# Order of work at the norms of a two-layer decoder trunk: hi products first, second transposes later, attention's delays 2.6/2.3 to 2.2/2.7

## The chip, the cores and the metric

The kernel runs on one core of one Trainium2 chip. The metric is the time of one execution on the device, in microseconds (us). TensorE (PE) does the products, VectorE (DVE) and ScalarE (ACT) the elementwise work, GpSimd (POOL) some small vector work, and SyncE (SP) issues most DMA transfers. "PEld" is TensorE's weight load, which runs beside its products.

## The reference, cut to what matters

The trunk has two layers over 256 tokens of width 1024. Each layer is an FFN, a mixer and a second FFN, each followed by a residual and a layer norm:

```
for l in range(DEPTH):                       # DEPTH = 2, x: (256, 1024) float32
    h = swiglu(x, w1[l,0], w3[l,0], w2[l,0]);  x = layernorm(ALPHA*x + 0.5*h)
    h = mixer(x, l, ...);                      x = layernorm(ALPHA*x + h)
    h = swiglu(x, w1[l,1], w3[l,1], w2[l,1]);  x = layernorm(ALPHA*x + 0.5*h)
```

`swiglu` is `(silu(x @ w1) * (x @ w3)) @ w2` with a hidden width of 2816. The mixer projects x to seven parts of width 1024 (u, v, q, k, val and two gates), runs a chunked spatial gate on u and v and a differential attention (8 heads, two score maps of head dimension 64 each, their difference applied to values of width 128) on q, k and val, and merges both through gates and two more weight matrices.

## The kernel before, in words

**Arithmetic.** Every float32 operand of a large product is split into a hi part, a reduced-precision copy that ScalarE writes, and a lo part, the rest, that VectorE writes. A product is then three: w_hi by x_hi, w_lo by x_hi, w_hi by x_lo. `three` (L271) issues them in that order. There x is the stationary operand (a 128x128 weight load for each product) and 512 columns of a weight matrix stream past it. `rows_b` does this for two slices of 128 along the contraction: six products, in the order hi-hi, lo-hi, hi-lo for the first slice, then the same for the second.

**A norm.** The tokens lie in two blocks of 128 (t = 0, 1), each with two halves of 512 columns (h = 0, 1). `finish_s` ends the statistics of a block and normalises it on VectorE (L556, second half first). The half h = 1 goes through ScalarE's `planes` (L184) and a DMA transpose on SP's queue (L189) to the tile `sent`; the half h = 0 goes through four transposes on TensorE (L633). `turn` then scales on ScalarE (L638, after a copy at L628 for h = 1), writes the hi part of x (ScalarE, L233) and the lo part (VectorE, L234), each for four slices of 128 in one instruction. The products of the next stage use x as soon as both are there: `gemm_b2` runs t = 0 with h = 0, then t = 0 with h = 1, then t = 1 in the same way, 24 products for each of these four. Five norms are followed by another stage: three that end an FFN and two that end a mixer. The sixth ends the kernel.

**What sets the order.** TensorE's order is that of the program text (`manual_schedule`). Side work is placed in it by a count of beats: each group of products adds to a clock (`beat`: 0.5 for six products of `rows_b`, and in `gemm_a2` 0.65 for eight of 512 columns and 0.35 for eight of 256), and a task, a generator, runs on when the clock has reached the time that its last `yield` asked for. `turned` is such a task: `waits[0]` beats after the norm of its block it does h = 0 (the four transposes), and `waits[1]` beats after that h = 1. On the other engines a planner orders the instructions: it simulates the engines and gives a free engine the most urgent of its instructions that is ready, where urgency follows the program text (`soon` raises it) and `behind` pins an instruction after another one on its engine.

**Attention.** The mixer computes q and k for two heads at a time (`rope`, four pairs `hp`, each q or k a `gemm_a2` of 2 beats), and after them the gates (eight more `gemm_a2`). Beside them runs, for each pair, the task `attend`, 3.9 beats after its k: scores of the second token block (L838), 0.6 beats later the scores of the first, their softmax (L846, L848) and the difference of the two maps (L857), then a delay, the transposes of the weights on TensorE (L872, L877) and their copies (L874, L879), a second delay, the products with the values (L885, L887), a copy (L890) and four squares (L895) on ScalarE that read and write the PSUM bank, then on GpSimd the norm's inverse root and later a packing and a DMA transpose. These small products share four PSUM banks (`side`).

Of the kernel before, what the change touches and what calls it, by code (L numbers as in the profile page):

```python
# [20 lines left out]
P = 128  # L21
# [3 lines left out]
KT = D // P  # L25
# [33 lines left out]
def trunk(ctx, tc, x, xT, w13a, w13b, w2s, w2p, wb, wqk, wa, wbr, wo, gateb, sgug, sgub, sguwT, sgubias, lam, diffg,  # L59
          lng, lnb, lngT, lnbT, cosT, sinT, out):  # L60
    nc = tc.nc
    V, A, G, PE = nc.vector, nc.scalar, nc.gpsimd, nc.tensor
# [19 lines left out]
    def bank():  # L82
        return psum.tile([P, 512], F32, tag="main", name=name("bank"))

    def side_bank():
        return psum.tile([P, 512], F32, tag="side", name=name("sbank"))
# [12 lines left out]
    def parts(f):  # L99
        return (lambda k: f(k)[:, :T]), (lambda k: f(k)[:, T:])  # L100
# [27 lines left out]
    def beat(w):  # L128

        clock[0] += w  # L130
        for task in list(tasks):
            if task[0] <= clock[0]:
                turn(task)

    def turn(task):
        try:
            task[0] = clock[0] + next(task[1])
        except StopIteration:
            tasks.remove(task)
# [11 lines left out]
    def behind(ins):  # L151

        return tc.issue_after(ins) if ins is not None else nullcontext()

    def stream(src, width=CH, sub=HC, lent=(), after=(None, None)):

        step()
        raw = raw_pool.tile([P, CH], F32, tag="raw", name=name("raw"))  # L160
        nc.sync.dma_start(raw[:, :width], src)
        out = []
        for o in range(0, width, HC):
            if o // HC in lent:
                hi, lo = ([act.tile([P, 512], F32R, tag="slot", name=name(n)) for _ in range(2)] for n in ("lhi", "llo"))
                at = [(hi[j], lo[j]) for j in range(2)]
            else:
                hi = hi_pool.tile([P, HC], F32R, tag="hi", name=name("whi"))
                lo = lo_pool.tile([P, HC], F32R, tag="lo", name=name("wlo"))
                at = [(hi[:, p : p + sub], lo[:, p : p + sub]) for p in range(0, HC, sub)]  # L170
            for p, (h, w) in zip(range(0, HC, sub), at):
                r = raw[:, o + p : o + p + sub]
                with behind(latest[0] if o // HC in lent else early[0] or latest[0]):
                    copied = A.activation(h, r, AF.Copy)  # L174
                if o // HC in lent:
                    early[0] = copied.ins
                with behind(after[o // HC] or latest[1]):
                    V.tensor_tensor(out=w, in0=r, in1=h.bitcast(F32), op=ALU.subtract)  # L178
            out.append((hi, lo))
        return out  # L180
# [37 lines left out]
    def rest_of(pre, after):  # L218

        (_, hi0, lo0), (raw, hi1, lo1) = pre  # L220
        lows(pre[1], after)
        hi = hi_pool.tile([P, HC], F32R, tag="hi", name=name("whi"))
        lo = lo_pool.tile([P, HC], F32R, tag="lo", name=name("wlo"))
        for p in range(0, HC, 512):
            r, h, w = (v[:, o + p : o + p + 512] for v, o in ((raw, HC), (hi, 0), (lo, 0)))
            with behind(early[0]):
                A.activation(h, r, AF.Copy)
            with behind(after):
                V.tensor_tensor(out=w, in0=r, in1=h.bitcast(F32), op=ALU.subtract)
        return [(hi0[:2], lo0[:2]), (hi0[2:], lo0[2:])], [(hi1, lo1), (hi, lo)]  # L230
# [37 lines left out]
    def three(ps, xh, xl, w_hi, w_lo, start, stop):  # L268

        for n, (w, xx) in enumerate([(w_hi, xh), (w_lo, xh), (w_hi, xl)]):  # L270
            PE.matmul(ps, xx, w, start=start and n == 0, stop=stop and n == 2)  # L271
# [30 lines left out]
    def rows_b(ps, t, k0, piece, xh, xl, kts, c0=0, n=512):  # L302

        hi, lo = piece
        for j in range(2):
            k, o = k0 + j, j * 512 + c0
            wh, wl = (w[j][:, c0 : c0 + n] if isinstance(w, list) else w[:, o : o + n] for w in (hi, lo))
            three(ps[:, :n], xh(k)[:, t * P : (t + 1) * P], xl(k)[:, t * P : (t + 1) * P], wh, wl,
                  k == 0, k == kts - 1)
        beat(n / 1024)  # L310

    def rows_p(ps, t, q, piece, xh, xl, c0=0, n=512, stop=False, start=False):

        for j, k in enumerate(q):
            wh, wl = (v[:, j * 512 + c0 : j * 512 + c0 + n] for v in piece)
            three(ps[:, :n], xh(k)[:, t * P : (t + 1) * P], xl(k)[:, t * P : (t + 1) * P], wh, wl,
                  start and j == 0, stop and j == 1)
        beat(n / 1024)
# [58 lines left out]
    def gemm_b2(srcs, xh, xl, done, norm=None):  # L377

        lent, after = [()] * 4, [(None, None)] * 4
        if norm:
            lent = [(0, 1), (0,), (), ()]
            after[1:3] = [(norm.ends[0], norm.ends[0])] * 2
        ps = [[bank() for _ in range(2)] for _ in range(NT)]
        got = [[None] * 4 for _ in range(2)]
        for t in range(NT):
            for c in range(2):
                if norm:
                    norm.ready(t, c)  # L390
                    after[3] = [norm.ends[1]] * 2
                for m in range(2):
                    n = 2 * c + m
                    if t == 0 and n < 2 and norm and norm.pre:
                        if n == 0:
                            got[0][:2], got[1][:2] = rest_of(norm.pre, norm.ends[0])
                    elif t == 0:
                        got[m][2 * c : 2 * c + 2] = stream(srcs[m][:, c * CH : (c + 1) * CH], sub=512, lent=lent[n],
                                                           after=after[n])
                    for i in range(2 * c, 2 * c + 2):  # L400
                        rows_b(ps[t][m], t, 2 * i, got[m][i], xh, xl, KT)
            early[0] = None
            with behind(latest[0] if t == 0 else None):
                done(t, ps[t])
# [246 lines left out]
    def ffn(l, f, i, norm, following=None):  # L651
# [59 lines left out]
        if norm is None:  # L711
            gemm_first([w13b[l, f, 0, 0], w13b[l, f, 1, 0]], front(0))
        else:
            gemm_b2([w13b[l, f, 0, 0], w13b[l, f, 1, 0]], xh, xl, front(0), norm=norm)
# [17 lines left out]
        def plain_pair(n):  # L732
            q = PQ[n]
            w = stream(w2p[l, f, n])
            for c in range(2):
                for t in range(NT):
                    for ps, o, m in ends[t, c]:
                        rows_p(ps, t, q, w[c], hh, hl, o, m, start=q == PQ[0] and t + c == 2)
# [50 lines left out]
    def mixer(l, i, norm):  # L789
        xh, xl = parts(both)  # L790
# [5 lines left out]
        def got_val(t, ps):  # L796
            for h in range(2):
                A.activation(val[t][:, h], ps[h], AF.Copy)

        gemm_b2([wb[l, VAL_, 0], wb[l, VAL_, 1]], xh, xl, got_val, norm=norm)  # L800

        hb = slots("hb", 2 * KT, F32R)
# [21 lines left out]
        def attend(hp, qT, kT):  # L824
# [27 lines left out]
            def less(t, pp):  # L852

                nk = (t + 1) * P
                for j in range(2):
                    s = slice(j * nk, (j + 1) * nk)
                    V.scalar_tensor_tensor(out=pp[0][:, s], in0=pp[1][:, s], scalar=c4[:, t * 2 + j : t * 2 + j + 1],  # L857
                                            in1=pp[0][:, s], op0=ALU.mult, op1=ALU.add)
                return pp[0]
# [4 lines left out]
            V.reciprocal(out=rc, in_=sums[:, 4:])  # L864
            V.scalar_tensor_tensor(out=c4, in0=rc, scalar=neg_lam[l], in1=sums[:, :4], op0=ALU.mult, op1=ALU.mult)
            second, first = less(1, second), less(0, first)
            yield 2.6
            b = side_bank()
            for j in range(2):
                for c in range(2):  # L870
# [6 lines left out]
                PE.transpose(b[:, j * P : (j + 1) * P], first[:, j * P : (j + 1) * P], ident)  # L877
            aT0 = slots("aT", 2)[0][:, :T]
            A.activation(aT0, b[:, :T], AF.Copy)  # L879
            yield 2.3  # L880
            b = side_bank()
            for j in range(2):
                h = hp * 2 + j
# [9 lines left out]
            for q in range(4):  # L893
                s = slice(q * P, (q + 1) * P)
# [8 lines left out]
            for q in range(4):  # L903
                t, j = q // 2, q % 2
# [9 lines left out]
            for j in range(2):  # L914
                h, s = hb[hp * 2 + j], slice(j * T, (j + 1) * T)
# [10 lines left out]
        for br, sec in ((0, GA_), (1, GB_)):  # L926
            gt = slots("gate", KT)
            gates.append(gt)
            for c in range(KT // 2):
                (_, b), = gemm_a2([wa[l, sec, c]], both, lambda m: t512("gz"), lambda: t512("r"))  # L930
                for n in range(2):
                    s = slice(n * T, (n + 1) * T)
# [11 lines left out]
        for t in range(NT):  # L944
# [3 lines left out]
            for h in range(2):  # L948
                s = slice(h * 512, h * 512 + 512)
# [5 lines left out]
        for h in range(2):  # L955
            s = slice(h * 512, h * 512 + 512)
# [46 lines left out]
        ln = Norm(l, i, 2.0 * ALPHA, 4.0 * EPS, m[:, :1])  # L1003

        def done(t, ps):
            for h in range(2):
                ln.part_s(t, h, ps[h], ln.scale)
            ln.finish_s(t, ((2, 1.5), (2, 1))[t])

        gemm_b2([wo[l, 0], wo[l, 1]], view(m_hi), view(m_lo), done)  # L1010
        return ln.close()

    norm = None
    for l in range(DEPTH):
        norm = ffn(l, 0, 0, norm, [wb[l, 1, m] for m in range(2)])
        norm = mixer(l, 1, norm)
        norm = ffn(l, 1, 2, norm, [w13b[l + 1, 0, m, 0] for m in range(2)] if l < DEPTH - 1 else None)
# [92 lines left out]
```

## Time and profile before

| | |
|---|---|
| median of 3 runs | 1212.65 us (1212.43 to 1213.14) |
| the profiled execution: its own time, its span | 1212.84 us, 1211.1 us |
| TensorE busy, products | 1204.1 us, 99% of the span, 5985 products |
| weight loads busy | 1013.1 us, 84% |
| VectorE busy | 944.3 us, 78% |
| ScalarE busy | 857.3 us, 71% |
| GpSimd busy | 91.7 us, 8% |
| moved by DMA | 257.01 MB, 212 GB/s on average |
| granted TensorE clock | full |

How to read it: times in the trace count from the start of the span. Busy shares are over the whole span. Products overlap in the pipeline, so a row of one product of 512 columns shows 0.39 us while such products follow one another more closely. In a row of the timeline stand start, length, engine, line, operation, output and inputs, shapes, the number of merged instructions, and in brackets the idle time ahead of it with what ended it. Engine names that end in q are a sequencer's.

### The profile page before, as it was taken

How to read it: one execution, taken by the hardware profiler on the slowest of the kernel's cores; microseconds unless marked ns; L12 is line 12 of the kernel's file. 1: busy time of each engine (PE TensorE's matmuls, PEld its weight loads, DVE VectorE, ACT ScalarE, POOL GpSimd, SP SyncE). 2: the span in 40 equal slices, each digit the busy share in tenths (PEclk: the TensorE clock that was granted, in tenths of full speed). 3: DMA queues.
4: the chain of work that ended last, by engine and by line, in shares of the span. 5: the costliest groups of instructions: out<-in, count | busy, mean ns of one | idle time of the engine just before them, and what ended most of it. 6: DMA issues, size and time to landing. Idle time of an engine off the chain costs nothing.

```text
span 1211.1 us, 16587 instructions
## 1 busy us (share of the span) xinstructions
PE 1204.1 (99%) x5985; PEld 1013.1 (84%) x5985; DVE 944.3 (78%) x1541; ACT 857.3 (71%) x1384; POOL 91.7 (8%) x184
## 2 busy tenths in 40 slices
PE   9999999999999999999999999999999999999998
PEld 8888888888888878888888888888888888888886
DVE  6658998885796876579985679989756877757798
ACT  6677677679865596776776776776897555767761
POOL 0100000233300000000000000003432000000000
PEclk9999999999999999999999999999999999999999
DMA  8985665655764658566667565765648546687551
GB/s 321 319 265 174 210 251 203 232 176 162 237 223 168 217 165 295 191 187 218 232 215 270 194 180 209 252 226 194 213 141 274 180 174 217 186 275 209 179 203 52
DMA packets 101347, 257.01 MB, mean 212 GB/s; under 512 B 66528, under 2 KB 67600, under 8 KB 74640
## 3 DMA queue, kind: packets, MB, share of 16 engines
q1 hardware_dynamic: 97296, 243.03, 59.9%
q0 software_dynamic: 3536, 12.13, 3.1%
q8 instruction: 47, 0.77, 0.2%
q10 hardware_dynamic: 432, 0.79, 0.2%
q14 instruction: 36, 0.29, 0.1%
HBM read 235.47 MB, written 1.05 MB: 195 GB/s over the span
## 4 chain that ended last, share of the span: by engine, by line
PE 93%; DVE 4%; ACT 2%; issue 1%; DMA 0%; DVEq 0%; ACTq 0%
PE bank L271 35%; PE sbank L271 23%; PE bank L283 17%; PE bank L290 9%; PE sbank L283 2%; PE bank L446 2%; PE sbank L290 1%; PE sbank L838 1%; PE sbank L970 1%; PE sbank L887 1%; DVE nwa L248 0%; ACT xf L638 0%; DVE xtok L556 0%; ACT sq L553 0%; DVE nwy L249 0%
## 5 line engine op out<-in xcount | busy, mean ns | idle before, releaser
L178 DVE TENSOR_TENSOR wlo<-raw,whi 128x1024 fp32r<-128x1024 f32 (+1 forms) x396 | 436.7, 1124 | 144.2 <-ACT whi L174 113.5
L174 ACT ACTIVATE whi<-raw 128x1024 fp32r<-128x1024 f32 (+1 forms) x396 | 372.9, 971 | 125.9 <-PE bank L283 43.3
L271 PE MATMUL bank<-whi,x 128*128 128x512 f32 x840 | 263.4, 390 | 0.0
L271 PEld LDWEIGHTS bank<-whi,x 128*128 128x128 f32 x840 | 157.7, 188 | 32.7
L271 PE MATMUL bank<-wlo,x 128*128 128x512 f32 x420 | 163.6, 390 | 0.0
L271 PE MATMUL sbank<-whi,x 128*128 128x512 f32 x512 | 159.0, 389 | 0.0
L283 PE MATMUL bank<-x,whi 128*128 128x512 f32 x640 | 156.0, 394 | 0.0
L283 PEld LDWEIGHTS bank<-x,whi 128*128 128x128 f32 x640 | 117.2, 188 | 26.3 <-issue 2.3
L271 PEld LDWEIGHTS sbank<-whi,x 128*128 128x128 f32 x512 | 96.1, 188 | 19.9
L353 ACT ACTIVATE shi<-raw 128x1024 fp32r<-128x1024 f32 (+1 forms) x80 | 73.4, 947 | 51.7 <-DVE raw L368 26.4
L271 PE MATMUL sbank<-wlo,x 128*128 128x512 f32 x256 | 99.7, 389 | 0.0
L355 DVE TENSOR_TENSOR slo<-raw,shi 128x1024 fp32r<-128x1024 f32 (+1 forms) x80 | 85.3, 1088 | 14.1 <-ACT shi L353 13.1
L271 PEld LDWEIGHTS bank<-wlo,x 128*128 128x128 f32 x420 | 78.9, 188 | 16.1
L290 PE MATMUL bank<-x,wlo 128*128 128x256 f32 x640 | 85.9, 285 | 0.0
L290 PEld LDWEIGHTS bank<-x,wlo 128*128 128x128 f32 x640 | 81.6, 191 | 2.2
L291 ACT ACTIVATE r<-bank 128x256 f32<-128x256 f32 x112 | 41.5, 376 | 24.7 <-PE bank L290 24.7
L271 PEld LDWEIGHTS sbank<-wlo,x 128*128 128x128 f32 x256 | 48.1, 188 | 9.9
L506 POOL DMA_DIRECT2D bc<-in_lng x6 | 3.2, 529 | 697.0 <-DVE bc L505 697.0
L271 PE MATMUL sbank<-whi,hhi 128*128 128x512 f32 (+1 forms) x144 | 55.5, 386 | 0.0
L271 PE MATMUL sbank<-whi,hlo 128*128 128x512 f32 (+1 forms) x144 | 55.3, 384 | 0.0
L271 PE MATMUL sbank<-wlo,hhi 128*128 128x512 f32 (+1 forms) x144 | 55.2, 384 | 0.0
L702 ACT ACTIVATE planes<-silu 128x1024 uint16<-128x1024 uint16 x40 | 42.0, 1054 | 7.3 <-DVE silu L701 6.2
(248 smaller groups left out, 2012.2 us busy)
## 6 DMA issues: line engine op xcount, KB each, us to landing
raw<-in_w13b SPq DMA_DIRECT2D x76, 1024.0 KB, 5.6
raw<-in_w2p SPq DMA_DIRECT2D x24, 1024.0 KB, 4.8
raw<-in_wa SPq DMA_DIRECT2D x24, 1024.0 KB, 5.3
raw<-in_w2s SPq DMA_DIRECT2D x20, 1024.0 KB, 4.8
raw<-in_wb SPq DMA_DIRECT2D x16, 1024.0 KB, 5.1
raw<-in_wqk SPq DMA_DIRECT2D x16, 1024.0 KB, 4.8
raw<-in_wbr SPq DMA_DIRECT2D x16, 1024.0 KB, 4.9
raw<-in_w13a SPq DMA_DIRECT2D x8, 1024.0 KB, 4.8
```

What stands on the lines that cost most here:

```text
L174: copied = A.activation(h, r, AF.Copy)
L178: V.tensor_tensor(out=w, in0=r, in1=h.bitcast(F32), op=ALU.subtract)
L271: PE.matmul(ps, xx, w, start=start and n == 0, stop=stop and n == 2)
L283: PE.matmul(b[-1], hi[:, k * P : (k + 1) * P], xc(k), start=k == 0, stop=False)
L290: PE.matmul(b[n][:, :T], lo[:, k * P : (k + 1) * P], xc(k)[:, :T], start=False, stop=k == KT - 1)
L291: emptied[0] = A.activation(r[:, s], b[n][:, T:], AF.Copy, scale=scale).ins
L353: A.activation(h, r, AF.Copy)
L355: V.tensor_tensor(out=w, in0=r, in1=h.bitcast(F32), op=ALU.subtract)
L446: PE.matmul(ps[t][m], x[:, j, o + t * P : o + (t + 1) * P], y, start=k0 + j == 0 and o == 0 and y is hi, stop=k0 + j == KT - 1 and y is lo)
L702: A.activation(pk.rearrange("p (w k) -> p w k", w=2), s.bitcast(U16).rearrange("p (k w) -> p w k", w=2), AF.Copy)
L838: PE.matmul(banks[m][:, j * nk : (j + 1) * nk], rows(qT, m, j, t * P, P), rows(kT, m, j, 0, nk), start=True, stop=True)
L887: PE.matmul(b[:, T + j * P : T + (j + 1) * P], aT1[:, (j * 2 + c) * P : (j * 2 + c + 1) * P], v[c], start=c == 0, stop=c == 1)
```

## The change

Three edits. First, at the five norms with a following stage, the first two groups of products (t = 0, the first matrix, slices 0 and 1, then 2 and 3) are issued by a new function: four products with x's hi part (hi and lo weights of both slices), then two with x's lo part. The products are the same twelve. Second, the mixers' norm gives its second block the delays 2.5 and 0.5 beats instead of 2 and 1; the FFNs' norms keep 2 and 1. Third, in `attend` the delay ahead of the transposes is 2.2 beats instead of 2.6, and the one between transposes and values 2.7 instead of 2.3.

```
+    def rows_hl(ps, t, k0, piece, xh, xl, kts):
+        for low in range(2):
+            for j in range(2):
+                k, s = k0 + j, slice(j * 512, (j + 1) * 512)
+                wh, wl = (w[j] if isinstance(w, list) else w[:, s] for w in piece)
+                for w in (wh,) if low else (wh, wl):
+                    PE.matmul(ps, (xh, xl)[low](k)[:, t * P : (t + 1) * P], w, start=not low and k == 0 and w is wh,
+                              stop=False)
+        beat(0.5)
...
     gemm_b2:
-                        rows_b(ps[t][m], t, 2 * i, got[m][i], xh, xl, KT)
+                        (rows_hl if norm and t + n == 0 else rows_b)(ps[t][m], t, 2 * i, got[m][i], xh, xl, KT)
...
     attend:
             second, first = less(1, second), less(0, first)
-            yield 2.6
+            yield 2.2
             b = side_bank()
...
             A.activation(aT0, b[:, :T], AF.Copy)
-            yield 2.3
+            yield 2.7
             b = side_bank()
...
     mixer, done:
-            ln.finish_s(t, ((2, 1.5), (2, 1))[t])
+            ln.finish_s(t, ((2, 1.5), (2.5, 0.5))[t])
```

## The prediction

> **What bounds the kernel now.** I read the page first, then the chain of waits, then the waits that end on TensorE, then the five places where one stage hands its normalised tokens to the next.
>
> ```profile
> span 1211.1 us, 16587 instructions
> ...
> PE 1204.1 (99%) x5985; PEld 1013.1 (84%) x5985; DVE 944.3 (78%) x1541; ACT 857.3 (71%) x1384; POOL 91.7 (8%) x184
> ...
> PE 93%; DVE 4%; ACT 2%; issue 1%; DMA 0%; DVEq 0%; ACTq 0%
> ```
> ```profile
> 28.06 21.76 PE sbank L271 x96
> ```
> ```profile
> PEld bank L271 <- DVE x L234: 2.7, 5, 0.6
> ```
> ```profile
>   DVE xtok L556: 2.1, 4
> ```
>
> The first fence is the page: TensorE is busy for 99% of the span and carries 93% of the chain. The second is a row of the chain: 96 products of 512 columns in 21.76 us, so 0.227 us for one. The third comes from the list of waits: five times TensorE's weight load waits for x's lo part, once at each norm. The fourth is what L633's transposes waited for: the normalised tokens, at two norms (twice each, as weight load and as product). So the end is set by TensorE's own work plus small stalls, and a change of order can earn only stalls.
>
> **The change, part by part.**
>
> *Hi products first.* At the first norm that a mixer follows:
>
> ```profile
> 182.95 0.42 PE L271 MATMUL bank<-lhi,x 128*128 128x512 f32 x1
> 183.06 0.68 DVE L234 TENSOR_TENSOR x<-xf,x 128x512 fp32r<-128x512 f32 x1
> 183.21 0.40 PE L271 MATMUL bank<-llo,x 128*128 128x512 f32 x1
> ...
> 183.79 0.30 PEld L271 LDWEIGHTS bank<-lhi,x 128*128 128x128 f32 x2 [0.62 <-DVE x L234]
> ...
> 187.56 0.39 PE L271 MATMUL bank<-whi,x 128*128 128x512 f32 x1
> ```
>
> Two products with x's hi part run; the third has x's lo part as its weights, and that is not written before 183.06 + 0.68 = 183.74. From 182.95 to 187.56 lie 18 products: 4.61 us where 18 x 0.227 = 4.08 would do, 0.53 lost. Counted back from 187.56 by 16 products, the third really began at 183.93. In the new order lo stands fifth and is due at 182.98 + 4 x 0.227 = 183.89, 0.04 before it can start. Of the 0.53 some 0.08 stays: 0.45 gained. The fourth product now needs the second weight's lo part, which was written before the norm. The list of waits has five such waits, three at norms that an FFN ends.
>
> At a norm that a mixer ends:
>
> ```profile
> 426.38 0.69 DVE L234 TENSOR_TENSOR x<-xf,x 128x512 fp32r<-128x512 f32 x1 [1.43 <-ACT x L233]
> 426.40 0.50 PE L271 MATMUL bank<-lhi,x 128*128 128x512 f32 x1
> ...
> 427.13 0.72 PE L271 MATMUL bank<-lhi,x 128*128 128x512 f32 x2
> ...
> 430.90 0.39 PE L271 MATMUL bank<-whi,x 128*128 128x512 f32 x1
> ```
>
> 18 products take 4.50, 0.42 too long. The first of them is 0.50 long instead of 0.39: 0.11 is a wait for hi, which stays. The other 0.30 is the wait for lo, shorter than the 0.45 by which lo is put off: gained whole.
>
> *The second transposes.* An FFN's norm, then a mixer's:
>
> ```profile
> 188.85 1.00 DVE L556 TENSOR_SCALAR xtok<-xtok,mv,nwy 128x512 f32<-128x512 f32 x2
> ...
> 190.06 0.58 PEld L633 LDWEIGHTS sbank<-ident,xtok 128*128 128x128 f32 x4
> ...
> 190.64 0.49 PE L271 MATMUL bank<-whi,x 128*128 128x512 f32 x1
> ```
> ```profile
> 433.05 1.00 DVE L556 TENSOR_SCALAR xtok<-xtok,mv,nwy 128x512 f32<-128x512 f32 x2
> 433.40 0.39 PE L271 MATMUL bank<-whi,x 128*128 128x512 f32 x1
> ...
> 434.11 0.42 PEld L633 LDWEIGHTS sbank<-ident,xtok 128*128 128x128 f32 x4 [0.74 <-DVE xtok L556]
> ...
> 434.52 0.48 PE L271 MATMUL bank<-whi,x 128*128 128x512 f32 x1
> ```
>
> Undisturbed, the next product follows 0.58 after the transposes' weight load (190.06 to 190.64). In the mixer the load could have begun with the product at 433.40 and the next product came at 434.52, 1.12 later: 0.54 is stall; I take 0.53. The load was 0.71 late, so 0.17 of lateness is absorbed. Half a beat is one group of six products, 1.36 us: the load comes to 433.40 - 0.30 + 1.36 = 434.46, after the 434.11 at which it could start. The stall goes. The total delay of the turn's other half is the same (2.5 + 0.5 = 2 + 1), and that half has no transposes on TensorE.
>
> The FFNs' delays are not changed, and there the first edit makes a new wait: the load comes at 190.06 - 0.45 = 189.61, the tokens are ready at 189.85 + 0.05 = 189.90. Of 0.29 lateness 0.17 is absorbed: 0.12 lost. Behind it on TensorE are only the products of the same norm.
>
> *What is late next in the mixers.* The moved transposes feed the second token block:
>
> ```profile
> 434.80 1.50 ACT L638 ACTIVATE xf<-sbank,ln_b,ln_g 128x128 f32<-128x128 f32 x4
> 436.34 0.63 ACT L233 ACTIVATE x<-xf 128x512 fp32r<-128x512 f32 x1
> 438.28 1.19 ACT L628 ACTIVATE xf<-sent 128x1024 uint16<-128x1024 uint16 x1 [1.31 <-DMA sent<-planes]
> ```
> ```profile
> 438.72 0.39 PE L271 MATMUL bank<-lhi,x 128*128 128x512 f32 x1
> ```
> ```profile
> 1038.73 1.19 ACT L628 ACTIVATE xf<-sent 128x1024 uint16<-128x1024 uint16 x1 [2.82 <-DMA sent<-planes]
> ```
> ```profile
> 1042.30 0.69 DVE L234 TENSOR_TENSOR x<-xf,x 128x512 fp32r<-128x512 f32 x1 [5.67 <-ACT x L233]
> ```
> ```profile
> 1042.87 0.62 PE L271 MATMUL bank<-whi,x 128*128 128x512 f32 x2
> ```
>
> Hi was ready at 436.97, 2.86 after the load at 434.11; after a load at 434.46 it is ready at 437.3, or 437.5 if the longer lag of the FFN holds. TensorE gets to 438.72 - 0.83 = 437.89: 0.4 to 0.6 to spare, and lo, 0.7 later, is just in time. The other half of the block comes through a DMA transpose. In the second layer its lo part ends at 1042.99; its first user is the second product of the last row, at 1043.10, and the first that needs lo stands at 1043.55. With TensorE 0.83 earlier that is 1042.72, but by the lag of the first fence (183.74 to 183.93) lo serves from 1043.18: 0.45 given back. In the first layer the copy comes 1.5 earlier against the same work, and nothing is lost.
>
> *Attention.* TensorE's order is a list of beats: 0.65 for eight products of 512 columns, 0.35 for eight of 256, and a due task runs at the first beat that reaches its time. I added the beats in code order. The first part's end stands at 8.65 beats; +2.6 makes 11.25 and +2.2 makes 10.85, and both are first reached at 11.30. So the transposes do not move at all. The values move instead: from 13.65 (11.30 + 2.3 = 13.60) to 14.00 in the second layer, and in the first, where the floating-point sum falls a hair short of the due time, to 14.65. They hold a PSUM bank until ScalarE has squared it, and two pairs of heads later the scores want it:
>
> ```profile
> 257.31 1.14 PE L838 MATMUL sbank<-qk,qk 64*128 64x256 f32 x8
> ```
> ```profile
> 263.98 0.39 PE L885 MATMUL sbank<-val,aT 128*128 128x128 f32 x2
> ```
> ```profile
> 269.44 0.59 ACT L890 ACTIVATE on<-sbank 128x512 f32<-128x512 f32 x1
> ...
> 272.82 0.26 ACT L895 ACTIVATE sbank<-sbank 128x128 f32<-128x128 f32 x1
> ```
> ```profile
> 272.59 1.80 PE L838 MATMUL sbank<-qk,qk 64*128 64x256 f32 x8
> ```
>
> The scores at 272.59 took 1.80 instead of 1.14: 0.66 lost to the last square. The values before them were done about 265.2, yet their copy went at 269.44 behind another pair's work. Values one beat later (2.77 us, about 268.0) with a copy at once, or one 1.05 us copy later, end their squares between 271.8 and 273.2, as copy to last square takes 3.8: the stall falls to something between 0 and 0.66. By the same lag the pair before it, whose scores at 257.31 wait for nothing, could lose up to 0.7. Bounds of the part: 0.66 gained to 0.7 lost. I take 0.2 gained, as the only wait that the trace shows is one that can shrink.
>
> *The sum.* Three FFN norms: 3 x (0.45 - 0.12) = 1.0. Two mixer norms: 2 x (0.30 + 0.53) - 0.45 = 1.2. Attention 0.2. Together 2.4. The profiled execution took 1212.84 (span 1211.1, 1.7 around it), so 1210.4; it stands 0.2 above the median of the runs, 1212.65, so I forecast **1210.25**.
>
> A page speaks against part of it. The Trainium skill, "DMA: Bandwidth & Descriptors", section "Issuing engines are not separate DMA queues", says that transfers from all engines run on the same 16 DMA engines and interleave. The rows behind it:
>
> ```profile
> 434.70:438.30 3.60, 3.60 (x18) 2.94 (x17) 2.45 (x4) 2.15 (x6) 0.00 (x0) 1.00 1.20 323
> ```
> ```profile
> DMA to landing us min/median/max: 2.7/2.7/5.0
> ```
>
> While the mixer's transpose is in flight the DMA engines carry 323 GB/s (last column of the stretch), and the ten transposes land after 2.7 to 5.0 us. The trace agrees with the page: the 0.45 is a matter of what the transpose meets. With the median landing it is nothing and the sum 2.85; with 5.0 in both layers it is paid twice and the sum is 1.95.
>
> **The rivals.**
>
> *Slower: ScalarE's order at the mixers flips.* ScalarE's instructions are put in order by a planner that fills a gap with whatever it holds ready. For the first block it put the copy of the DMA transpose (L628) right behind the four scalings (L638), ahead of hi:
>
> ```profile
> 420.23 1.06 ACT L184 ACTIVATE planes<-xtok 128x1024 uint16<-128x1024 uint16 x1 [2.73 <-DVE xtok L556]
> ...
> 424.65 1.18 ACT L628 ACTIVATE xf<-sent 128x1024 uint16<-128x1024 uint16 x1
> ```
> ```profile
> 433.63 1.06 ACT L184 ACTIVATE planes<-xtok 128x1024 uint16<-128x1024 uint16 x1 [0.44 <-DVE xtok L556]
> ```
>
> That was 4.4 us after the packing (L184) began; for the second block hi went first, 2.7 after it (433.63 to 436.34). With later transposes that moment comes at about 3.2. If the planner believes the transpose landed by then, L628 goes ahead of hi, and it really waits until 438.28 and 1038.73. Hi then starts at 439.5 and 1039.9 and serves at about 440.3 and 1040.8, where TensorE stands from 437.89 and 1036.8 (the same work 598.9 later, less 0.83): 2.4 and 3.9, with 0.25 more each for lo, 6.8 lost against 2.85 gained elsewhere. The time would be 1212.65 + 4 = 1216.6. Against it: 1.1 for packing plus the median 2.7 makes 3.8, more than 3.2. It decides from there: 15%.
>
> The Trainium skill, "TensorE: Matmul & The Clock Gate", section "What's actually happening", says that an idle window of about 3.4 us halves TensorE's clock. No stall of this trace is that long, so no run shows it here; the longer of the two stalls would reach it, and an estimate by that page adds up to 1.7 us, 1218.3.
>
> *Everything earned.* The transposes land early, the tokens of the FFN norms come before the load, and attention loses its 0.66: 3 x 0.45 + 2 x 0.83 + 0.66 = 3.7, 1209.0. For it: the landing varies. Against: L556 ends when VectorE gets there, and nothing in the change moves it. 10%.
>
> *Given back.* Reordered lists on ScalarE and VectorE make a stall of the size now removed, and the bank wait of attention doubles: 2.4, less 0.7 + 0.2 for attention, less about 1.0 for one norm-sized stall in each layer, leaves 0.5, 1212.15. For it: margins of 0.1 to 0.6 in two places. 15%.
>
> *The change does not do what it says.* For the attention part this is in the forecast; its transposes stay.
>
> **How the numbers follow.** The forecast has 60%, its own range 1209.4 to 1211.3 from the bounds of attention and of the landing. A measurement of this kernel tells about 0.2%, 2.4 us, from no change, so the forecast lies on that edge and is split half and half: faster 0.30 + 0.10 = 0.40, same 0.30 + 0.15 = 0.45, slower 0.15. The range runs from below "everything earned" to above "given back", 1208.9 to 1213.2, and leaves out the slower case.
>
> **What would show it.** Right: no wait for L234 ahead of the third product and the fifth within 0.1; L633 in the mixers without a wait, in the FFNs with about 0.1; attention's transposes behind the same products as now, values one group later in the second layer and two in the first. Wrong: L628 ahead of L233 for the second block, a wait of the scores near 257, or a gap of TensorE that none of these rows has.

## The result, and the profile after

The changed kernel takes 1220.5 us (median of 6 runs, 1219.9 to 1221.5) against 1212.5 us (1211.9 to 1213.1): 8.0 us slower, ratio 1.0068 with a 95% interval of 1.0058 to 1.0078. The forecast was 1210.25 us with a range up to 1213.2.

The first lines of the page of the changed kernel, and its shares of the chain of waits:

```profile
span 1218.2 us, 16590 instructions
...
PE 1203.9 (99%) x5985; PEld 1013.0 (83%) x5985; DVE 943.2 (77%) x1541; ACT 856.7 (70%) x1384; POOL 85.4 (7%) x184
...
PE 96%; DMA 1%; ACT 1%; DVE 1%; POOL 1%; SPq 0%; issue 0%; DVEq 0%; ACTq 0%; POOLq 0%
```

These lines hide the loss. TensorE is as busy as before to 0.2 us, and its share of the chain has even risen; but DMA and POOL, which had at most a rounded 0% of the chain before, now have 1% each. The list of waits that end on TensorE's weight loads shows where (total, times, longest):

```profile
PEld sbank L849 <- ACT aT L885: 8.1, 1, 8.1
```

One wait of 8 us, once. L849 are attention's scores (L838 before), and L885 is the copy of a pair's transposed weights (L874 before), which empties a PSUM bank. TensorE's timeline there, in layer 1, at the scores of the fourth pair:

```profile
271.83 0.70 PE L849 MATMUL sbank<-qk,qk 64*128 64x256 f32 x2
280.22 2.07 PE L849 MATMUL sbank<-qk,qk 64*128 64x256 f32 x6 [7.69 <-ACT aT L885]
...
284.98 0.72 PE L849 MATMUL sbank<-qk,qk 64*128 64x128 f32 x8
```

Before, the same products stood at 272.59 and took 1.80. A measure that holds for all kernels here is the time from the start of this pair's first scores to the start of its second ones. Undisturbed it is 3.13 us (in layer 2 before: 872.14 to 875.27). In layer 1 it was 3.76 before (272.59 to 276.35) and is 13.15 now: 9.4 us lost. The norms gained 2.1 us (below). That leaves 7.3, and the span grew by 7.1.

The chain of waits, followed back from these scores (start, duration, what):

```profile
262.25 5.30 DMA swap<-z
...
267.71 1.79 POOL swap L825
269.50 0.17 POOL ss L909
...
274.98 0.69 ACT both L917 x2
...
277.99 0.95 ACT both L184
...
279.21 0.48 ACT on L901
279.69 0.49 ACT aT L885
280.22 2.07 PE sbank L849 x6
```

Read forwards: a transfer for the rotary embedding of the fourth pair's k lands, GpSimd multiplies it (L825), and only then does GpSimd begin the inverse root of the *first* pair (L909, then 14 operations until 274.94). ScalarE's list has that pair's four scalings (L917) and its packing (L184) ahead of the copies of the second pair's values (L901) and of the third pair's transposed weights (L885), and the last one empties the bank that the fourth pair's scores want.

ScalarE's own timeline, with the idle time before an instruction in brackets:

```profile
269.69 0.21 ACT L903 ACTIVATE s<-sums 128x4 f32<-128x4 f32 x1 [1.96 <-POOL ss L909]
274.98 0.69 ACT L917 ACTIVATE both<-on,nwy 128x128 f32<-128x128 f32 x2 [5.08 <-POOL nwy L264]
```

ScalarE stood still for 7.04 us with ready work behind it. GpSimd and ScalarE before, at the same place:

```profile
259.92 0.20 POOL L898 TENSOR_TENSOR ss<-s,ss 128x4 f32<-128x4 f32 x1
...
265.67 0.20 POOL L264 TENSOR_TENSOR nwy<-nwa,nwy 128x4 f32<-128x4 f32 x1
265.85 1.30 POOL L814 TENSOR_TENSOR swap<-swap,sin_t 128x512 f32<-128x512 f32 x1
```
```profile
266.90 1.27 ACT L906 ACTIVATE both<-on,nwy 128x128 f32<-128x128 f32 x4
...
273.11 0.58 ACT L874 ACTIVATE aT<-sbank 128x512 f32<-128x512 f32 x1
```

ScalarE's order (scalings, copy of the values, copy of the transposed weights) was the same before. What is new is that GpSimd's inverse root comes 9.5 us later, 269.46 instead of 259.92: behind the last rotary product instead of ahead of it. Some 1.9 us of this are the rotary product itself, which stood at 265.85 before and at 267.71 now: SyncE issued its transfer at 258.45 before and at 260.42 now. Why it did so was not traced.

**The theory** from this: the values run one beat later in layer 1, so the code that follows them in the task is issued one beat later too. `behind(turned_by[0])` ties the inverse root to the rotary product that was issued last, and one beat later that is the next one. GpSimd is late, ScalarE's queue waits behind the scalings, the bank stays full, and the scores stop. **Rivals:** the values' own bank, held until its squares (the prediction's bank wait); or the new order at the norms, which shifts every list behind it.

### The profile page after: what moved, and what is told of

The parts are those of the page before. It is cut to its first block, busy times and chain, and to the rows that moved or that the text cites. A ratio compares the mean times of both kernels' runs of the same rounds, so it can differ in the third digit from the quotient of the medians.

```text
span 1218.2 us, 16590 instructions
## 1 busy us (share of the span) xinstructions
PE 1203.9 (99%) x5985; PEld 1013.0 (83%) x5985; DVE 943.2 (77%) x1541; ACT 856.7 (70%) x1384; POOL 85.4 (7%) x184
## 4 chain that ended last, share of the span: by engine, by line
PE 96%; DMA 1%; ACT 1%; DVE 1%; POOL 1%; SPq 0%; issue 0%; DVEq 0%; ACTq 0%; POOLq 0%
PE bank L271 37%; PE sbank L271 25%; PE bank L283 16%; PE bank L290 8%; PE sbank L283 2%; PE bank L457 2%; PE sbank L290 1%; PE bank L319 1%; PE sbank L849 1%; DMA swap<-z 1%; PE sbank L981 1%; PE sbank L898 0%; PE sbank L644 0%; SPq L821 0%; DVE wlo L178 0%
## 5 line engine op out<-in xcount | busy, mean ns | idle before, releaser
L174 ACT ACTIVATE whi<-raw 128x1024 fp32r<-128x1024 f32 (+1 forms) x396 | 373.1, 970 | 126.3 <-PE bank L283 41.4
L283 PE MATMUL bank<-x,whi 128*128 128x512 f32 x640 | 158.2, 397 | 0.0
L283 PEld LDWEIGHTS bank<-x,whi 128*128 128x128 f32 x640 | 117.4, 189 | 26.6 <-issue 2.3
```

Of the source, the lines that this page charges most:

```text
L283: PE.matmul(b[-1], hi[:, k * P : (k + 1) * P], xc(k), start=k == 0, stop=False)
```

## The experiments

Times with their ratio to the kernel before on the same chip. The column "norms" is the time lost in the 96 products of each of the five norms, over 0.227 us for each product and 0.35 for a set of transposes, summed. "Scores" is the measure above, in layer 1 and layer 2 (undisturbed 3.13). Both are from the one profiled execution.

| kernel | us | ratio (95%) | norms | scores |
|---|---|---|---|---|
| before | 1212.5 | 1 | 4.17 | 3.76, 3.13 |
| after | 1220.5 | 1.0068 (1.0058 to 1.0078) | 2.03 | 13.15, 3.22 |
| norms_only | 1213.1 | 1.0004 (0.9995 to 1.0012) | 1.61 | 6.36, 4.28 |
| attn_only | 1222.75 | 1.0084 (1.0069 to 1.0100) | 4.11 | 13.25, 3.18 |
| pool_free | 1216.55 | 1.0030 (1.0018 to 1.0042) | 1.55 | 5.32, 6.78 |
| scale_later | 1210.3 | 0.9982 (0.9973 to 0.9991) | 2.10 | 3.67, 3.14 |
| two_groups | 1230.55 | 1.0144 (1.0128 to 1.0159) | not worked out | 14.07, 15.35 |
| one_group | 1210.4 | 0.9985 (0.9976 to 0.9994) | 1.59 | 3.80, 3.82 |
| hl_only | 1213.7 | 1.0013 (1.0004 to 1.0022) | 3.11 | 4.95, 4.25 |
| late_only | 1211.6 | 0.9994 (0.9985 to 1.0002) | 3.23 | 3.38, 3.75 |
| best_a | 1210.1 | 0.9980 (0.9971 to 0.9989) | 2.02 | 3.13, 3.13 |

**attn_only: the attention edit by itself.** Against the kernel before:

```
-            yield 2.6
+            yield 2.2
...
-            yield 2.3
+            yield 2.7
```

> The kernel before with attention's two delays alone changed to 2.2 and 2.7. Theory: the whole stall is here, without the gains at the norms: 1212.5 + 8.1 - 0.7 (the stall of before at the same scores goes) + 2.2 (products at half clock behind it) = 1222.1, ratio 1.008. Rival (the stall needs the norms' new order as well): 1212 to 1213.

It took 1222.75 us. The stall is here without any change at the norms:

```profile
272.55 0.70 PE L838 MATMUL sbank<-qk,qk 64*128 64x256 f32 x2
280.09 2.07 PE L838 MATMUL sbank<-qk,qk 64*128 64x256 f32 x6 [6.84 <-ACT aT L874]
```

The theory's number holds within 0.7 us, and the rival that needs the norms' new order falls.

**scale_later: only ScalarE's list.** Against the changed kernel, after the inverse root:

```
             r = rsqrt4(ss, 1.0 / (2 * HD))
-            yield 2
+            yield 3.2
```

> The changed kernel, in which the delay between a pair's inverse root and its scaling by it is 3.2 beats instead of 2. The values stay late, and GpSimd's inverse root of the first pair stays behind the rotary product (ends about 275 us); but ScalarE's instruction list now has the copy of the next pair's values and the copies of the transposed weights ahead of the four scalings. Theory (what stalls TensorE is the place of the scalings in ScalarE's list): the inverse root is as late as in the changed kernel, the scores wait less than 1.5 us (ScalarE still waits some 2 us for the first addition if the square of the sums stays ahead of the copies), 1210 to 1212.5. Rival (the inverse root's lateness stalls whatever stands in the list, or the values' bank does): 1218 to 1221.

It took 1210.3 us. GpSimd's timeline and then ScalarE's:

```profile
265.83 1.45 POOL L825 TENSOR_TENSOR swap<-swap,sin_t 128x512 f32<-128x512 f32 x1 [6.70 <-DMA swap<-z]
267.25 0.38 POOL L909 TENSOR_TENSOR ss<-s,ss 128x4 f32<-128x4 f32 x1
...
273.74 0.20 POOL L264 TENSOR_TENSOR nwy<-nwa,nwy 128x4 f32<-128x4 f32 x1
```
```profile
271.62 0.58 ACT L885 ACTIVATE aT<-sbank 128x512 f32<-128x512 f32 x1
...
274.97 1.29 ACT L917 ACTIVATE both<-on,nwy 128x128 f32<-128x128 f32 x4
```

The inverse root is tied behind the same rotary product and ends at 273.94, 1.0 us ahead of the changed kernel's and 8.1 us behind that of the kernel before. But the scalings now stand behind the copy of the transposed weights, which ends at 272.20, and the scores wait for half a microsecond. So neither GpSimd's lateness alone nor the later values make the long stall: it takes the scalings ahead of the copy in ScalarE's queue. The rival that the values' own bank makes it falls too, as the values are as late here.

**pool_free: only GpSimd's order.** Against the changed kernel the tie is taken out:

```
-            with behind(turned_by[0]):
-                G.tensor_tensor(out=ss, in0=s2, in1=ss, op=ALU.add)
+            G.tensor_tensor(out=ss, in0=s2, in1=ss, op=ALU.add)
```

> The changed kernel, in which the first addition of a pair's inverse root on GpSimd is no longer tied behind the last rotary product that was issued before it (the tie and nothing else is taken out). The values stay as late as in the changed kernel; on GpSimd the inverse root of the first pair now stands ahead of the two rotary products that it had to follow. Theory (values one beat later make the inverse root be issued after the next rotary product and so be tied behind it; ScalarE's queue waits for it ahead of the copy that frees the scores' bank): the addition runs at about 257 to 260 us instead of 269.5, the scores of the fourth pair in layer 1 wait less than 1 us, 1220.5 - 10 = 1210 to 1211.5. Rival (the later values hold their own bank, whatever GpSimd does): the stall of about 8 us stays, 1220.5.

It took 1216.55 us, 5 more than expected. GpSimd did what was meant, with the values still late:

```profile
256.44 0.22 POOL L908 TENSOR_TENSOR ss<-s,ss 128x4 f32<-128x4 f32 x1 [9.05 <-ACT sbank L906]
...
262.84 0.49 POOL L264 TENSOR_TENSOR nwy<-nwa,nwy 128x4 f32<-128x4 f32 x1
```

The wait of 8 us shrank to 1.5 at the same scores, but did not go below 1, and a second one came up in layer 2. TensorE in layer 1, ScalarE ahead of it, and TensorE in layer 2:

```profile
273.67 1.13 PE L849 MATMUL sbank<-qk,qk 64*128 64x256 f32 x6 [1.52 <-ACT aT L885]
```
```profile
269.84 1.05 ACT L184 ACTIVATE both<-both 128x1024 uint16<-128x1024 uint16 x1
...
271.61 1.04 ACT L174 ACTIVATE whi<-raw 128x1024 fp32r<-128x1024 f32 x1
...
273.03 0.58 ACT L885 ACTIVATE aT<-sbank 128x512 f32<-128x512 f32 x1
```
```profile
873.71 1.65 PE L849 MATMUL sbank<-qk,qk 64*128 64x256 f32 x6 [1.42 <-ACT aT L885]
```

The tie makes the large stall. What is left is ScalarE's list: it no longer waits, but runs the scalings, two weight copies (L174) and the packing (L184) ahead of the copy that the scores need.

**two_groups and one_group: where the values fall.** Against the changed kernel, the second delay alone:

```
-            yield 2.7
+            yield 2.75        (two_groups)
+            yield 2.69        (one_group)
```

With 2.7 the values fall on 14.65 beats in layer 1 and 14.00 in layer 2; with 2.75 on 14.65 in both, with 2.69 on 14.00 in both. In layer 1 their products start at 266.01 in the changed kernel, behind eight more products of L283, and at 264.00 with 2.69, ahead of these.

> The changed kernel with the values' delay 2.75 instead of 2.7, so that the values fall on 14.65 beats in the second layer as well (in the changed kernel they stand there at 14.00). Theory (a group later, the inverse root is tied behind the next rotary product): the stall of 8 us with its half clock comes a second time, in layer 2: 1220.5 + 8 to 10 = 1228.5 to 1230.5. Rival (the stall is an accident of the first layer): 1220 to 1222.

> The changed kernel with the values' delay 2.69 instead of 2.7: in both layers the values then fall on 14.00 beats, half a group later than before and half a group earlier than the changed kernel's first layer. Theory (from 14.00 the inverse root is still issued ahead of the next rotary product and not tied behind it; only at 14.65 is it late): the 8 us stall is gone and both layers look like the changed kernel's second: 1220.5 - 10 = 1210.5; up to 1213 if ScalarE's list puts a weight copy ahead of the transposed weights' copy as with the norms' edits alone. Rival (any move of the values costs the stall): 1218 to 1221.

They took 1230.55 and 1210.4 us. At two_groups the second layer stalls as well, and at one_group the first no longer does (1.83 us for its scores, 1.14 undisturbed):

```profile
890.06 2.07 PE L849 MATMUL sbank<-qk,qk 64*128 64x256 f32 x6 [8.94 <-ACT aT L885]
```
```profile
271.67 1.83 PE L849 MATMUL sbank<-qk,qk 64*128 64x256 f32 x8
```

A hundredth of a beat in a constant is worth 10 us in one layer, and five hundredths the other way cost 10 in the other. The step between 14.00 and 14.65 decides, as the theory has it.

**norms_only: both edits at the norms, attention as before.** (Against the changed kernel the two delays are put back to 2.6 and 2.3.)

> The changed kernel with attention's two delays put back to 2.6 and 2.3; the order of hi and lo and the mixers' later transposes stay. Theory (all of the loss is one stall of 8.06 us in layer 1's attention and the half clock behind it): no stall above 0.7 us, the products of the five norms as in the changed kernel, 2.1 us less lost there than in the kernel before: 1210.4, ratio 0.998. Rival (the new order at the norms shifts the planner's lists and so carries a part of the loss): above 1212.5, and if it carries all of it 1220.

It took 1213.1 us: no gain. The norms gained even more than expected (4.17 to 1.61), but the scores lost it again, in both layers. Layer 1, TensorE and then ScalarE:

```profile
271.37 0.70 PE L849 MATMUL sbank<-qk,qk 64*128 64x256 f32 x2
273.21 1.13 PE L849 MATMUL sbank<-qk,qk 64*128 64x256 f32 x6 [1.15 <-ACT aT L885]
```
```profile
271.35 1.04 ACT L174 ACTIVATE whi<-raw 128x1024 fp32r<-128x1024 f32 x1
...
272.58 0.58 ACT L885 ACTIVATE aT<-sbank 128x512 f32<-128x512 f32 x1
```

The rival that I had set against it was right in kind: the planner made another list on ScalarE, with a weight copy and a square right ahead of the copy of the transposed weights, in a stage that the edit does not touch. That copy now starts 1.21 us after the scores do; before it was 0.52 (272.59 to 273.11). In the changed kernel the later values hid this loss under the larger one.

**hl_only and late_only: the two norm edits apart.** Against the kernel before, hl_only has `rows_hl` and the call of it, late_only this:

```
-            ln.finish_s(t, ((2, 1.5), (2, 1))[t])
+            ln.finish_s(t, ((2, 1.5), (2.5, 0.5))[t])
```

> The kernel before with the new order of hi and lo at the five norms and nothing else. Theory A (by the kernel with the norms' edits alone: the products at the norms gain 0.4 us each, but ScalarE's list in attention comes out in that kernel's new order, which costs some 1.2 us in the first layer, 0.6 in the second and in some executions 2 us of half clock): 1212.8 - 1.6 + 1.8 + 0 to 2.3 = 1213 to 1215, scores' stalls in both layers. Theory B (each edit earns what its own place shows, and the lists' shift comes from the mixers' delays): 1211.2.

> The kernel before with the second transposes of the mixers' norms half a beat later and nothing else. ScalarE's list in attention is here the one of before. Theory A: two stalls of 0.53 us go, the scores' stall in layer 1 stays at 0.7 us: 1212.8 - 1.06 = 1211.7, ratio 0.9991. Theory B (the lists' shift comes from this edit): 1213 or more.

hl_only took 1213.7 us, as theory A had it, with the same two waits as norms_only:

```profile
273.88 1.13 PE L849 MATMUL sbank<-qk,qk 64*128 64x256 f32 x6 [1.15 <-ACT aT L885]
```
```profile
434.70 0.42 PEld L644 LDWEIGHTS sbank<-ident,xtok 128*128 128x128 f32 x4 [0.99 <-DVE xtok L567]
```

The second fence is its first mixer's norm: the transposes wait longer for their tokens than before (0.74), and the two mixer norms lose 1.10 each as before (1.09). There hi first alone earns nothing. late_only took 1211.6 us; its interval reaches 1.0002, so the expected 0.9991 is consistent with it and no more. ScalarE's list around these scores comes out changed with hl_only and not with late_only. The list is not all that sets them: with the list of before, late_only lost 0.25 at the first layer's scores and 0.62 at the second's.

**best_a: the scalings out of the way, the values in their old place.** norms_only with the delay after the inverse root at 3.2 instead of 2:

> Both edits at the norms, attention's two delays as before (2.6 and 2.3), and the delay between the inverse root and the scaling by it 3.2 beats instead of 2. ScalarE's list then has the copy of the values right after a pair's exponentials, and the scalings behind the copies of the next pair's transposed weights. Theory (the place of the scalings in ScalarE's list sets the scores' wait): no wait of the scores over 0.2 us in either layer, no half clock, the norms' gain of 2.5 and the 0.7 us of before's stall: 1212.8 - 3.2 = 1209.6. Rival (the values' bank is the limit, and ScalarE is late there whatever comes first): 1211 to 1213.

It took 1210.1 us, 0.5 above what was expected, and the scores wait nowhere (1.13 us for the eight, as undisturbed):

```profile
271.80 1.13 PE L849 MATMUL sbank<-qk,qk 64*128 64x256 f32 x8
```

It is 2.4 us better than before; scale_later and one_group cannot be told from it.

## Why the prediction was wrong, step by step

**Hi products first: right.** Timeline of TensorE at the first norm of the changed kernel, first and nineteenth product, and at the first mixer's norm:

```profile
182.54 0.39 PE L319 MATMUL bank<-lhi,x 128*128 128x512 f32 x1
...
186.69 0.39 PE L271 MATMUL bank<-whi,x 128*128 128x512 f32 x1
```
```profile
435.04 0.50 PE L319 MATMUL bank<-lhi,x 128*128 128x512 f32 x1
...
439.27 0.39 PE L271 MATMUL bank<-whi,x 128*128 128x512 f32 x1
```

18 products take 4.15 and 4.23 us, where they took 4.61 and 4.50: 0.46 and 0.27 gained, 0.45 and 0.30 predicted. "Gained whole" at the mixers holds only together with the later transposes, as hl_only shows.

**The second transposes: right.** The new wait of the FFN norms cost 0.08 to 0.12 (0.12 predicted): the products around the transposes of the first norm start 0.69 apart instead of 0.58. In the mixers the stall is gone. In layer 2, 0.48 comes back at the last half (0.45 predicted). The norms together gained 2.14 in the changed kernel; 2.2 was forecast. That the 0.45 came true is partly luck: in norms_only, with the same edits at the norms, the copy of the DMA transpose starts 4.8 us after the packing instead of 6.2, and the 0.48 does not come back. Nor do the rows of the kernel before show that the landing follows the traffic: the transpose beside 323 GB/s was in after 3.6 us, and the one in layer 2, which took 5.0, met 257 GB/s.

**The slower rival: it did not happen.** ScalarE kept its order at the first mixer's norm:

```profile
445.53 0.63 ACT L233 ACTIVATE x<-xf 128x512 fp32r<-128x512 f32 x1
446.98 1.18 ACT L639 ACTIVATE xf<-sent 128x1024 uint16<-128x1024 uint16 x1 [0.82 <-DMA sent<-planes]
```

Hi goes ahead of the copy of the DMA transpose.

**Attention: the step that failed.** That the transposes stay and the values move by 0.35 beats in layer 2 and by a whole beat in layer 1 was right (two_groups and one_group turn the loss on and off with it). Wrong was the next sentence, "Bounds of the part: 0.66 gained to 0.7 lost", with its reason, "the only wait that the trace shows is one that can shrink". It bounded the move by the bank that the values themselves hold, and let the values' copy run at once, about 268.0, or one weight copy later. In the changed kernel the products with the values were done by 267.5 and their copy (L901) ran at 279.11. The prediction asked nothing of what is issued after the values in the same task: the inverse root, its tie to a rotary product, and the scalings that wait for it in ScalarE's queue, ahead of both copies. The loss was 9.4 us, and it shows by the sign that the prediction gave for being wrong, a gap of TensorE that none of its rows has.

The rows of the kernel before would have shown a stall of this size. The tie names the rotary product issued last. One beat later that is the one at 265.85, which ended at 267.15. The inverse root took from 259.92 to 265.87, 5.95 us: it would end at 273.1. From the scalings to the copy of the transposed weights ScalarE took from 266.90 to 273.11, 6.2 us: the copy would begin at 279.3. Scores that want its bank at 272.6 are then 6.7 us late. The trace after has the copy at 279.59. That the two agree to 0.3 us is luck, as three errors cancel: the rotary product ended at 269.50, 2.3 later than this working has it, the inverse root took 5.5, and ScalarE took 4.6 from the scalings to the copy.

**"Given back": right in kind, too small.** It named reordered lists on ScalarE and priced them at about 1.0 in each layer. norms_only lost 2.6 in layer 1 and 1.15 in layer 2 at the scores, against before, and with that the whole gain of the norms; 1.4 of the 2.6 are a half clock (last section). Without the attention edit the forecast would have missed by some 2.5 us (2.2 faster by its own terms, 0.3 slower measured), though inside its range.

**What stays open.** Why the planner's list on ScalarE in attention changes with the order of products at the norms was not traced; that it does is shown by hl_only, late_only and norms_only.

## What to carry to other kernels

When a step of a task is moved, follow everything that the task issues after it, on every engine, and look at what each of these is tied to and what stands behind it in an in-order queue: here an inverse root of 128x4 elements, further down the task and one beat later, cost 9.4 us. A tie to "whatever was issued last" changes its target in steps; work out on which side of the step a new delay falls, and keep away from its edge. And a gain at one place is only a gain if the lists that a planner makes elsewhere stay as they were, so compare those lists first.

## What the runs showed of the hardware that was not expected

TensorE's clock falls to half for stalls shorter than I had thought. The stretches of the changed kernel around the long wait (start and end, length, busy time of each engine, granted clock third from the right):

```profile
276.00:277.00 1.00, 0.00 (x0) 0.00 (x0) 0.00 (x0) 1.00 (x5) 0.00 (x0) 0.99 0.00 0
277.00:278.00 1.00, 0.00 (x0) 0.00 (x0) 0.00 (x0) 1.00 (x3) 0.00 (x0) 0.50 0.00 0
...
283.40:283.80 0.40, 0.40 (x3) 0.30 (x2) 0.00 (x0) 0.40 (x3) 0.26 (x2) 0.50 0.88 369
283.80:284.20 0.40, 0.40 (x4) 0.31 (x3) 0.00 (x0) 0.40 (x3) 0.32 (x2) 1.00 1.11 471
```

The clock is halved from 277.0, some 4.5 us after the last product, until 283.8, 3.6 us after the products went on. Of the 10.02 us over the undisturbed 3.13, 8.1 are the wait and some 1.9 the half clock. The Trainium skill, "TensorE: Matmul & The Clock Gate", section "What's actually happening", puts the halving after an idle window of about 3.4 us and the release after a busy one as long, in windows that run freely. The trace agrees with the Trainium skill there, and the prediction's estimate of 1.7 us by that section was near.

norms_only had waited for 1.15 us only:

```profile
271.40:273.20 1.80, 0.67 (x3) 0.26 (x2) 0.77 (x1) 1.80 (x6) 0.00 (x0) 1.00 0.83 259
273.20:274.60 1.40, 1.39 (x7) 0.97 (x8) 0.88 (x2) 1.40 (x5) 0.82 (x4) 0.99 0.93 392
274.60:277.70 3.10, 3.10 (x8) 1.98 (x6) 2.74 (x9) 2.14 (x7) 2.53 (x7) 0.50 0.35 50
```

It had its full clock during the wait and for 1.4 us after it, then half clock for 3.1 us under full load. hl_only, with the same wait of 1.15, kept its full clock:

```profile
275.00:276.00 1.00, 1.00 (x6) 0.82 (x6) 0.48 (x2) 1.00 (x3) 0.78 (x3) 1.00 0.28 98
276.00:277.00 1.00, 1.00 (x7) 0.56 (x5) 1.00 (x2) 0.26 (x1) 0.94 (x1) 1.00 0.00 0
```

It reached its second scores after 4.95 us where norms_only took 6.36. In pool_free both happened in one execution: the wait of 1.52 us in layer 1 left the clock at 1.00, and the one of 1.42 in layer 2 was followed by 0.50 from 875 to 877, and the second scores came after 6.78 us instead of 5.32. So a wait of a little over a microsecond has a further price, about 1.4 us, that comes or not; what decides is not shown. Here the measurement goes beyond what the Trainium skill states in that section: in norms_only TensorE was busy for 2.1 of the 3.2 us from 271.4 to 274.6, and no stretch of 3.4 us was idle.
